# A corrected table of transfer and copy durations in the planner that interleaves a hybrid decoder step's streams

## The chip, the cores and the metric

The kernel runs on one core of a Trainium2 chip. The metric is the device time of one execution in microseconds (us), given as the median of three runs. A separate profiled execution supplies the trace. Engines are named as the profile names them: PE is TensorE (PEld its weight loads), DVE is VectorE, ACT is ScalarE, POOL is GpSimd, and SP is the queue from which nearly all transfers (DMAs) are issued.

## The reference

One layer of a decoder trunk is computed for a prompt of 1024 tokens and for 8 single-token samples, all in float32, with a model width of 1024. In outline:

```python
def mixer_inputs(...):                       # one projection feeds two mixers
    h = rms_norm(x, norm_g) * (1.0 + scale) + shift          # scale, shift, gate = c @ w_ada + b_ada
    q, kv, nsa_g, z_a, u, v, z_b, g_a, g_b = jnp.split(h @ w_in, cuts, axis=-1)
    ...
def nsa_core(...):                           # mixer A: three attention branches
    p_c = softmax(q . kc) ; o_c = p_c @ vc                   # compressed blocks of 32 keys
    idx = top_k(block importance from p_c, 8) ; o_s          # 8 selected blocks of 64 keys
    o_w = softmax over the last 512 keys                     # sliding window
    ...
def spatial_mix(vn, w_s, b_s):               # mixer B: tril(w_s) @ v_norm + b_s inside chunks of 128
    ...
def mixer_output(...):
    o_a = gw[..., 0] * o_c + gw[..., 1] * o_s + gw[..., 2] * o_w      # per head, sigmoid gates
    a = (o_a * silu(z_a)) @ w_br_a
    b = (u * s_b * silu(z_b)) @ w_br_b
    m = sigmoid(g_a) * a + sigmoid(g_b) * b
    return x + gate * (m @ w_out)
```

The samples attend to paged caches of 1024 earlier tokens; the new key and value rows are outputs as well.

## The kernel before, in words

Each float32 operand of a large product is split into a high and a low half (names ending in `h` and `l`), and a product is the three matmuls high by high, low by high, and high by low. The order of all instructions is fixed while the program is built: no scheduler reorders anything afterwards, and on each engine and each queue the instructions run in the order in which they were written.

That order is set by a planner in the source, the class `Plan`. The kernel is written as about a dozen Python generators ("streams"), each of which emits some instructions and then yields, with the tile or the condition on which its next step depends. `Plan` keeps a modelled clock for each engine. `Plan.op` is called for every instruction. It takes the start as the engine's free time or the modelled end of the operands, whichever is later, adds a duration from the table in `Plan.cost`, and notes the end. For a transfer it moves a modelled bus forward by bytes over a rate and adds a latency. `Plan.go` repeatedly picks the stream whose awaited operand is ready earliest by these clocks, measured against PE's modelled clock, with a rank to break ties. Every instruction therefore shows one line in the profile, L231, the line in `Plan.engine` that passes a call on to the engine. Tiles are told apart by name.

The stages, in order of time:

1. Modulation and first projections (to about 250 us): weights are loaded as `graw`, split into `gh` and `gl`, and 128-token tiles `xt` are normalised, transposed through the PSUM bank `mx` and copied to `hx`.
2. The samples' attention ("decode", about 250 to 404 us): cache rows arrive in `gk`, are transposed into `mx` and copied to `kh`, `kl`.
3. The prompt's attention (about 404 to 810 us): 16 query tiles (two key groups by eight blocks of 128 queries). For each tile, a "front" transposes the split queries `s` into `mx`, copies them to `R` and `R2`, and computes score maxima: PE writes scores into `mx` (`mx<-L,R`) and DVE reduces them to `bm` and `wm`. Then come the scores (`st<-R,L`), the exponentials on ACT (`pt<-st`), their split (`p`), and the products with the values (`pv<-p,vv`), which I call P·V. A "close" ends each tile: ACT copies the softmax sum to `sr` and the output to `u`; a transfer spreads the sum into `s` (`s<-sr`); DVE takes its reciprocal; a transfer writes it out (`w_d<-s`), two read it back over the partitions (`f<-w_d`); POOL multiplies `u` by `f`; PE adds the compressed branch (`mx<-pgT,vc`); DVE sums (`u<-mx,u`), and two transfers store the result (`o_d<-u`). The runs of `sr`, `s` and `f` in these transfers are 32 or 512 bytes long.
4. The merge (about 810 to 965 us). Products `xh`, `xl` are made from the stored mixer rows, loaded as `zt`; they are the right-hand sides of the merge matmuls (`<-xh,c0h` and the like). The first merge group reads ten of the twelve products of branch b. The loading of `zt` begins once the last tile has been closed.
5. The output projection and the stores (to the end).

Alongside stages 2, 3 and the start of 4 runs a filler stream, `stream(jobs)`, of rank 9: 28 jobs of projections (gates, `z`, `u`) of three pieces each. A piece is 24 matmuls of 128x344 (`mm<-hh,c0h`, `mm<-hh,c0l`, `mm<-hl,c0h` and the same with `c1`), 84 pieces or 2016 matmuls in all; its result leaves by ACT (`th`) and a transfer (`t_da<-th`, `t_db<-th`). In stage 3 a pacing rule (`paced`) also limits how many pieces may have started for the share of the tiles that is done. What is left of the filler when the last tile closes runs ahead of the merge.

PSUM has two banks of each of the four tags `mm`, `st`, `pv`, `mx`. Transposes, score maxima and the compressed branch all share the two `mx` banks, so the next group in `mx` needs the reader of the group before the last to be done.

Of the kernel before, what the change touches and what calls it, by code (L numbers as in the profile page):

```python
# [11 lines left out]
BF = mybir.dt.bfloat16  # L12
# [4 lines left out]
PSUM = bass.MemoryType.PSUM  # L17
# [75 lines left out]
class Plan:  # L93
# [72 lines left out]
    def cost(self, engine, name, outs, ins, size, start):  # L166
        if engine == "pe":
            n, m, dt = ins[1].free_size(), ins[0].free_size(), ins[0].dtype
            form, passes, turn = "split", 1, 0.0
            if dt == FR and name != "transpose":  # L170
                cost = max(0.4375 * n + 7, 104 * m / 128)
                turn = {"split": 0.0, "full": 85.0, "part": 190.0}[self.form]
            elif name == "transpose" or dt == BF:
                form, passes = "full", 2 if name == "transpose" else 1
                cost = max(0.4375 * n + 7, (26 if dt == BF else 104) * m / 128)
                turn = 190.0 if self.form == "part" else 0.0
            elif m <= 64 and n > 128:
                form, passes, cost = "part", 4, 0.4375 * n * 4 * m / 128 + 3
                turn = 0.0 if self.form == "part" else 140.0
            else:  # L180
                form, passes, cost = "full", 4, max(4 * (0.4375 * n + 7), 208 * m / 128)
                turn = 190.0 if self.form == "part" else 0.0
            self.form = form
            tick = int(start // self.TICK)
            self.columns[tick] = self.columns.get(tick, 0.0) + passes * n * ins[0].partition_size() / 128
            return cost * (2 if self.cold(start) else 1) + turn
        if engine == "dve":
            plain = name == "tensor_copy" and outs[0].space == ins[0].space
            if name == "reciprocal":
                return 80 + 18 * size  # L190
            return 67 + (0.52 if plain else 1.042) * size
        if engine == "act":
            moved = ins and self.box(ins[0])[1][0] != self.box(outs[0])[1][0]
            return (280 if len(ins) > 1 else 70) + 0.834 * size + (105 if moved else 0)
        if name == "affine_select":
            return 65 + 1.4 * size
        if name == "tensor_scalar":
            return max(330 + 0.83 * size, 3.61 * size - 28)
        return (300 + 165 * size if size < 16 else 70 + 2.27 * size)

    def op(self, engine, name, outs, ins):
        size = max(x.free_size() for x in outs + ins)
        start = self.free.get(engine, 0.0)
        for x in ins:
            start = max(start, self.after(x, True, engine))
        for x in outs:
            start = max(start, self.after(x, False, engine))
        for x in ins + outs:
            if x.space == PSUM:
                start = max([start] + [y[2] for y in self.seen.get(self.box(x)[0], ()) if y[3] != engine])  # L210
        if "dma" in name:
            self.free[engine] = start + (1038.0 if engine == "pool" else 450.0)
            self.bus = max(self.bus, self.free[engine]) + outs[0].free_nbytes() * outs[0].partition_size() / 359.0
            end = self.bus + 2000.0
        else:
            cost = self.cost(engine, name, outs, ins, size, start)
            self.free[engine] = start + cost
            end = start + cost + self.LATE[engine]
            self.last = max(self.last, end + 60.0)
        for x in ins:  # L220
            self.note(x, False, end, engine)
        for x in outs:
            self.note(x, True, end, engine)
# [1812 lines left out]
```

## Time and profile before

| what | value |
|---|---|
| median of 3 runs | 1073.53 us (1072.48 to 1075.21) |
| profiled execution, own time | 1068.52 us |
| its span in the trace | 1066.8 us |
| PE busy | 1017.3 us (95%) |
| PE weight loads busy | 873.6 us (82%) |
| DVE busy | 697.2 us (65%) |
| ACT busy | 469.3 us (44%) |
| POOL busy | 308.8 us (29%) |
| mean granted TensorE clock | 0.994 |
| read from and written to memory | 98.95 MB, 30.23 MB |

The profiled execution took 5.0 us less than the median of the three runs, so a sum made inside the trace has to be carried over to the median as a difference. A duration in a timeline row covers a merged run of like instructions (x4 is four of them); the number in square brackets is how long the engine had sat idle before it and what released it. Matmuls overlap, so their spacing and not their single duration says what PE spends on one.

### The profile page before, as it was taken

How to read it: one execution, taken by the hardware profiler on the slowest of the kernel's cores; microseconds unless marked ns; L12 is line 12 of the kernel's file. 1: busy time of each engine (PE TensorE's matmuls, PEld its weight loads, DVE VectorE, ACT ScalarE, POOL GpSimd, SP SyncE). 2: the span in 40 equal slices, each digit the busy share in tenths (PEclk: the TensorE clock that was granted, in tenths of full speed). 3: DMA queues.
4: the chain of work that ended last, by engine and by line, in shares of the span. 5: the costliest groups of instructions: out<-in, count | busy, mean ns of one | idle time of the engine just before them, and what ended most of it. 6: DMA issues, size and time to landing. Idle time of an engine off the chain costs nothing. (4 is left out here: it accounts for less than half of the span.)

```text
span 1066.8 us, 16303 instructions
## 1 busy us (share of the span) xinstructions
PE 1017.3 (95%) x5587; PEld 873.6 (82%) x5587; DVE 697.2 (65%) x1507; ACT 469.3 (44%) x984; POOL 308.8 (29%) x332
## 2 busy tenths in 40 slices
PE   6899999998999999998988999999999999999998
PEld 2489987878999998887776877778789999998776
DVE  4685686445679674798888878988842354564422
ACT  4674232001323454677675776567674341232000
POOL 0462575554321100033342324433342000252000
PEclk9999999999999999999999999999999999999999
DMA  8736351203858563411220121211123666553521
GB/s 305 231 124 206 103 182 41 70 21 123 287 186 272 179 199 87 130 53 44 78 67 28 44 64 34 65 49 46 33 67 105 192 218 201 165 170 102 168 86 63
DMA packets 106311, 130.32 MB, mean 122 GB/s; under 512 B 27299, under 2 KB 71525, under 8 KB 106230
## 3 DMA queue, kind: packets, MB, share of 16 engines
q1 hardware_dynamic: 101622, 112.52, 33.7%
q0 software_dynamic: 4608, 16.78, 5.0%
q8 instruction: 44, 0.72, 0.3%
q14 instruction: 37, 0.30, 0.1%
HBM read 98.95 MB, written 30.23 MB: 121 GB/s over the span
## 5 line engine op out<-in xcount | busy, mean ns | idle before, releaser
L231 PE MATMUL pv<-p,vv 128*128 128x512 f32 (+1 forms) x396 | 111.4, 397 | 0.0
L231 ACT ACTIVATE pt<-st 128x512 f32<-128x512 f32 x132 | 78.5, 595 | 47.8 <-PE st L231 41.9
L231 PE MATMUL mm<-hh,c1h 128*128 128x344 f32 x304 | 99.5, 327 | 0.0
L231 PE MATMUL mm<-hh,c1l 128*128 128x344 f32 x304 | 97.7, 321 | 0.0
L231 PE MATMUL mm<-hl,c1h 128*128 128x344 f32 x304 | 97.7, 321 | 0.0
L231 PE MATMUL mm<-hh,c0h 128*128 128x344 f32 x296 | 96.4, 326 | 0.0
L231 PE MATMUL mm<-hh,c0l 128*128 128x344 f32 x296 | 94.6, 319 | 0.6 <-DVE c0l L231 0.6
L231 PE MATMUL mm<-hl,c0h 128*128 128x344 f32 x296 | 94.5, 319 | 0.0
L231 PE MATMUL st<-R,L 128*128 128x512 f32 (+1 forms) x264 | 86.2, 408 | 0.0
L231 PEld LDWEIGHTS pv<-p,vv 128*128 128x128 f32 (+1 forms) x396 | 66.0, 171 | 21.9 <-DVE p L231 1.5
L231 DVE TENSOR_TENSOR p<-pt,p 128x512 fp32r<-128x512 f32 x88 | 73.4, 844 | 11.2 <-ACT p L231 10.9
L231 POOL TENSOR_TENSOR p<-pt,p 128x512 fp32r<-128x512 f32 x44 | 60.1, 1366 | 62.2 <-ACT p L231 58.3
L231 PE MATMUL mx<-L,R 128*128 128x512 f32 (+3 forms) x204 | 56.6, 344 | 10.4 <-DVE wm L231 4.1
L231 ACT ACTIVATE p<-pt 128x512 fp32r<-128x512 f32 x94 | 59.1, 629 | 15.9 <-POOL pt L231 12.5
L231 PEld LDWEIGHTS mm<-hh,c1h 128*128 128x128 f32 x304 | 57.7, 190 | 2.4
L231 PEld LDWEIGHTS mm<-hh,c1l 128*128 128x128 f32 x304 | 57.6, 190 | 2.3
L231 POOL TENSOR_TENSOR m<-m,th 128x344 f32<-128x344 f32 x24 | 24.8, 1053 | 119.9 <-DMA th<-t_da 96.3
L231 POOL TENSOR_SCALAR_AFFINE_SELECT pt<-pt 128x512 f32<-128x512 f32 x40 | 27.1, 678 | 108.7 <-ACT pt L231 105.7
L231 PEld LDWEIGHTS mm<-hh,c0l 128*128 128x128 f32 x296 | 55.7, 188 | 3.3 <-DVE c0l L231 0.9
L231 PEld LDWEIGHTS mm<-hh,c0h 128*128 128x128 f32 x296 | 55.7, 188 | 2.8 <-issue 0.4
L231 PEld LDWEIGHTS mm<-hl,c1h 128*128 128x128 f32 x304 | 57.6, 189 | 0.0
L231 PEld LDWEIGHTS mx<-L,R 128*128 128x128 f32 x204 | 34.4, 188 | 26.7 <-PE mx L231 5.1
(517 smaller groups left out, 2753.0 us busy)
## 6 DMA issues: line engine op xcount, KB each, us to landing
t_db<-th SPq DMA_DIRECT2D x24, 172.0 KB
t_da<-th SPq DMA_DIRECT2D x24, 172.0 KB
th<-t_db SPq DMA_DIRECT2D x24, 172.0 KB
th<-t_da SPq DMA_DIRECT2D x24, 172.0 KB
graw<-in_w_ada_dram SPq DMA_DIRECT2D x16, 256.0 KB
araw<-in_w_ada_dram SPq DMA_DIRECT2D x16, 256.0 KB
xt<-in_x_dram SPq DMA_DIRECT2D x8, 512.0 KB
eraw<-in_w_ada_dram SPq DMA_DIRECT2D x16, 256.0 KB
```

Of the source, the lines that this page charges most:

```text
L231: r = getattr(real, name)(*args, **kw)
```

## The change

Two branches of the planner's table are altered. No instruction's operands are written differently; what the table does is to move the planner's choice of the next stream.

```diff
         if engine == "act":
-            moved = ins and self.box(ins[0])[1][0] != self.box(outs[0])[1][0]
-            return (280 if len(ins) > 1 else 70) + 0.834 * size + (105 if moved else 0)
+            if len(ins) > 1:
+                return 280 + 0.834 * size
+            p, space = outs[0].partition_size(), (ins or outs)[0].space
+            return (70 if space == PSUM else 94) + 0.834 * size + (105 if p < 128 and (p != 64 or size == 256) else 0)
...
         if "dma" in name:
-            self.free[engine] = start + (1038.0 if engine == "pool" else 450.0)
-            self.bus = max(self.bus, self.free[engine]) + outs[0].free_nbytes() * outs[0].partition_size() / 359.0
-            end = self.bus + 2000.0
+            self.free[engine] = start + (1038.0 if engine == "pool" else 500.0)
+            short = min(4 * x.ap[-1][1] for x in outs + ins[:1]) < 512
+            self.bus = max(self.bus, self.free[engine]) + outs[0].free_nbytes() * outs[0].partition_size() / (179.5 if short else 359.0)
+            end = self.bus + (4200.0 if short else 2200.0)
```

(The remaining lines of the diff write `7` as `7.0` in the PE branch, which changes no value.) In the table, in ns:

- an ACT copy of one input has a base of 70 from PSUM as before, and of 94 from SBUF (70 before);
- the extra 105 goes to copies onto fewer than 128 partitions, other than 64 partitions with a size that isn't 256; before, it went to copies that start on another partition than their source;
- issuing a transfer on SP takes 500 (450 before), and the fixed latency is 2200 (2000 before);
- a transfer whose innermost run on either side is under 512 bytes moves at half the rate and has a latency of 4200.

Both programs have the same number of instructions on each engine. What the new table moves is the order, at these places among others. The line numbers differ by three because the change adds three lines.

PE, the ninth group of transposes of `s` (its trace time before is 489.05 us). Before, it follows directly on another group in `mx`:

```order
L231 MATMUL st<-R,L_4360 128x512
L231 MATMUL st<-R_4912,L_4363 128x512
L231 MATMUL mx<-L_4360,R 128x512
L231 MATMUL mx<-main,s_5279 128x128 x4
L231 MATMUL st<-R,L_4360 128x512
```

Now:

```order
L234 MATMUL pv<-p_5433,vv_4366 128x512
L234 MATMUL mm<-hh,c0h 128x344
L234 MATMUL mm<-hh,c0l 128x344
L234 MATMUL mm<-hl,c0h 128x344
L234 MATMUL mm<-hh,c0h 128x344
L234 MATMUL mm<-hh,c0l 128x344
L234 MATMUL mm<-hl,c0h 128x344
L234 MATMUL mx<-main,s_5458 128x128 x4
L234 MATMUL st<-R,L_4360 128x512
```

Six filler matmuls and P·V now stand between the group in `mx` that came before and the transposes.

SP, the end of the attention: the read-back of the last tile's factor (`f<-w_d_4389`), the last store (`o_d<-u`), and the loads of the merge (`zt`). Before:

```order
L231 DMA o_d_94<-u 128x128
L231 DMA f<-w_d_4389 64x4x128 x2
L231 DMA t_da_137<-th 128x344 x2
L231 DMA o_d_93<-u 128x128
L231 DMA o_d_94<-u 128x128
L231 DMA zt<-z_db_130 128x344 x3
L231 DMA t_da_137<-th 128x344
L231 DMA cr<-in_w_ga_dram 128x512 x2
L231 DMA zt<-z_db_131 128x344
L231 DMA t_da_138<-th 128x344
L231 DMA zt<-z_db_131 128x344 x2
```

Now:

```order
L234 DMA o_d_94<-u 128x128
L234 DMA f<-w_d_4389 64x4x128 x2
L234 DMA t_da_139<-th 128x344
L234 DMA cr<-in_w_ga_dram 128x512 x2
L234 DMA t_da_140<-th 128x344
L234 DMA o_d_93<-u 128x128
L234 DMA o_d_94<-u 128x128
L234 DMA zt<-z_db_130 128x344 x3
L234 DMA t_da_140<-th 128x344
L234 DMA zt<-z_db_131 128x344
L234 DMA t_da_140<-th 128x344
L234 DMA cr<-in_w_br_b_dram 128x512 x2
```

`t_da` is numbered by job, so the last store now stands two to three jobs further on in the filler (among the rows of job 140 instead of job 137), and the first weights of the merge (`in_w_br_b`) follow almost at once. `f<-w_d` of the last tile stays behind the store of the tile before it.

ACT, in the first 25 us, where the split weights `gh` of the modulation and the turned tiles `hx` alternate. Before:

```order
L231 ACTIVATE hx,xss<-xt 128x1024
L231 ACTIVATE hx<-mx 128x512
L231 ACTIVATE gh<-graw 128x512 x3
L231 ACTIVATE mrow<-mm 9x512
L231 ACTIVATE hx<-mx 128x512
```

Now:

```order
L234 ACTIVATE hx,xss<-xt 128x1024
L234 ACTIVATE gh<-graw 128x512
L234 ACTIVATE hx<-mx 128x512
L234 ACTIVATE gh<-graw 128x512
L234 ACTIVATE hx<-mx 128x512
L234 ACTIVATE gh<-graw 128x512
L234 ACTIVATE mrow<-mm 9x512
```

One `gh` has moved ahead of `hx<-mx`, another in between the two, and the third behind them.

How far the filler has come at some points of the program, in matmuls of the 2016, counted in the order of PE:

| point in PE's order | before | now |
|---|---|---|
| end of the decode's values | 672 | 696 |
| first scores of the prompt | 888 | 936 |
| first scores of the last tile | 1584 | 1728 |
| last P·V | 1620 | 1764 |
| last close (`mx<-pgT,vc`) | 1710 | 1896 |
| first merge matmul | 2016 | 2016 |

Behind the last P·V stood 42 filler matmuls, the close of tile 15 of 16, 48 more, the close of the last tile, and then 306. Now there are 90, the close of tile 15, 42, the last close, and 120.

More of the change, by code (lines that the diff above doesn't have):

```diff
@@ L170, in cost @@
             if dt == FR and name != "transpose":
-                cost = max(0.4375 * n + 7, 104 * m / 128)
+                cost = max(0.4375 * n + 7.0, 104 * m / 128)
                 turn = {"split": 0.0, "full": 85.0, "part": 190.0}[self.form]
@@ L174, in cost @@
                 form, passes = "full", 2 if name == "transpose" else 1
-                cost = max(0.4375 * n + 7, (26 if dt == BF else 104) * m / 128)
+                cost = max(0.4375 * n + 7.0, (26 if dt == BF else 104) * m / 128)
                 turn = 190.0 if self.form == "part" else 0.0
@@ L180, in cost @@
             else:
-                form, passes, cost = "full", 4, max(4 * (0.4375 * n + 7), 208 * m / 128)
+                form, passes, cost = "full", 4, max(4 * (0.4375 * n + 7.0), 208 * m / 128)
                 turn = 190.0 if self.form == "part" else 0.0
```

## The prediction

> **What bounds the kernel now.** I read the page's totals first, then a table of busy time by stage, then PE's waits, and last the timeline where those waits are longest.
>
> ```profile
> span 1066.8 us, 16303 instructions
> ...
> PE 1017.3 (95%) x5587; PEld 873.6 (82%) x5587; DVE 697.2 (65%) x1507; ACT 469.3 (44%) x984; POOL 308.8 (29%) x332
> ```
>
> PE is busy for all but 49.5 us. Both programs hold the same instructions, so only that idle time can shrink or grow. The table by stage (from and to; length; busy time of PE, its weight loads, DVE, ACT, POOL; granted clock; DMA share; GB/s) tells where it lies:
>
> ```profile
> core 0: us, PE busy (x) PEld busy (x) DVE busy (x) ACT busy (x) POOL busy (x), PEclk, DMA share, GB/s
> 0.00:50.00 50.00, 38.78 (x130) 13.52 (x131) 27.81 (x59) 26.91 (x50) 12.07 (x19) 0.94 0.81 269
> 50.00:250.00 200.00, 198.41 (x1024) 169.20 (x1023) 126.07 (x298) 62.80 (x136) 104.03 (x103) 1.00 0.35 107
> 250.00:350.00 100.00, 95.43 (x615) 90.96 (x614) 71.97 (x105) 27.36 (x53) 30.41 (x30) 0.98 0.72 234
> ...
> 404.00:449.80 45.80, 42.09 (x272) 40.30 (x273) 25.43 (x67) 25.87 (x64) 1.87 (x7) 1.00 0.44 122
> 449.80:600.00 150.20, 137.66 (x734) 112.35 (x733) 132.92 (x322) 104.11 (x223) 52.16 (x60) 1.00 0.19 55
> 600.00:801.50 201.50, 192.09 (x1015) 158.81 (x1014) 161.27 (x375) 135.97 (x284) 72.74 (x78) 1.00 0.16 49
> 801.50:826.00 24.50, 24.50 (x154) 23.77 (x153) 6.44 (x11) 11.44 (x23) 6.72 (x9) 1.00 0.38 114
> 826.00:881.40 55.40, 55.40 (x354) 55.40 (x354) 23.76 (x46) 20.83 (x45) 0.18 (x1) 1.00 0.66 202
> 881.40:975.00 93.60, 92.57 (x568) 90.23 (x567) 52.57 (x95) 22.32 (x31) 24.78 (x24) 1.00 0.53 162
> ```
>
> Length less PE busy gives 11.2 us of idle time at the start, 4.6 in the decode's first part, and 3.7, 12.5 and 9.4 in the prompt's attention, together 25.6. From 801.5 to 881.4, where leftover filler runs on without a break, there is none.
>
> What ends these waits (in all, times, longest):
>
> ```profile
> PE mx L231 <- DVE bm L231: 8.7, 12, 2.3
> PE mx L231 <- DVE wm L231: 7.3, 15, 0.8
> PE mm L231 <- ACT gh L231: 7.3, 3, 5.6
> ```
>
> The attention's waits are mostly on DVE, which reduces score maxima out of one of the two `mx` banks while PE wants it for something else. Three of them on PE:
>
> ```profile
> 489.05 0.63 PE L231 MATMUL mx<-main,s 128*128 128x128 f32 x4 [0.46 <-DVE bm L231]
> ...
> 560.75 0.41 PE L231 MATMUL mx<-main,s 128*128 128x128 f32 x2 [2.30 <-DVE bm L231]
> ...
> 687.65 0.63 PE L231 MATMUL mx<-main,s 128*128 128x128 f32 x4 [0.78 <-DVE wm L231]
> ```
>
> DVE ahead of the longest:
>
> ```profile
> 557.31 2.37 DVE L231 TENSOR_TENSOR p<-pt,p 128x512 fp32r<-128x512 f32 x2
> 559.60 0.28 DVE L231 TENSOR_TENSOR mx<-mx,tri 128x128 f32<-128x128 f32 x1
> 559.92 0.69 DVE L231 TENSOR_REDUCE bm<-mx 128x8 f32<-128x512 f32 x1
> ```
>
> The maximum that PE needed stood behind two splits of `p`. PE work placed ahead of such a transpose hides the wait; where another group in `mx` comes directly before it, nothing does.
>
> **The change, as a sum.** The table's numbers only steer the order, so I cost the order. A filler matmul takes 55.40 / 354 = 0.157 us, by the row 826.00:881.40. By the list in the section on the change, 144 of them, 22.5 us, move from behind the last P·V to ahead of it. The stretch ahead grows by 22.5 us less the idle time they fill; the stretch behind shrinks by 22.5 us plus any new wait. The 22.5 cancels, so the result is minus the idle time filled, plus new waits. Four terms:
>
> *Start.* One `gh` moves ahead of `hx` on ACT:
>
> ```profile
> 20.25 0.60 ACT L231 ACTIVATE hx<-mx 128x512 f32<-128x512 f32 x1 [3.18 <-PE mx L231]
> 20.74 1.66 ACT L231 ACTIVATE gh<-graw 128x512 fp32r<-128x512 f32 x3
> ...
> 21.41 0.43 PE L231 MATMUL mm<-gh,cs 128*42 128x512 f32 x1 [0.83 <-ACT gh L231]
> ```
>
> PE's wait of 0.83 shortens by the 0.49 between the two ACT starts. The ends are -0.8 (the wait gone) and +1.7 (a later `hx` or `mrow` waiting for all three `gh`). I take -0.5: the rest of this stage's idle time waits for the first weights, which come as before.
>
> *Decode.* Its two longest waits stand before transposes of gathered rows:
>
> ```profile
> 264.92 0.63 PE L231 MATMUL mx<-main,gk 128*128 128x128 f32 x4 [2.50 <-DVE red L231]
> ...
> 281.71 0.52 PE L231 MATMUL mx<-main,gk 128*128 128x128 f32 x3 [0.93 <-DMA gk<-in_cache_k_slc_dram,idx]
> ```
>
> The new order has 42 filler matmuls where 36 stood before the first of these, 0.94 us, and 12 more before a later group. That fills 0.94 and about half of the 0.93. I take -1.5, with ends 0 and -3.4 (both waits gone).
>
> *Attention.* The filler between the first scores and the first scores of the last tile grows from 696 matmuls to 792. Does it land where PE waits? Of the 24 groups of transposes of `s`, 11 stand directly behind another group in `mx` before, and 6 now; the one at 489.05 is such a place. For each group in `mx` I also summed, from the order, the PE work since the last use of its bank. DVE needs 0.28 + 0.69 us for a mask and a reduction, plus its queue, so I call a bank covered with 1.5 to 2 us of PE work. What is missing up to 1.5 us sums to 18.3 us before and 11.6 now (37% less); up to 2 us, 46.7 and 37.6 (19.5% less). Scaling the stage's 25.6 us of idle time by these gives -9.4 and -5.0 as ends. I take -6.5, nearer the weaker one, since a wait like that at 560.75 comes from DVE's queue and moves with it.
>
> *Start of the merge.* Here cover is taken away. The chain behind the last P·V (PE, SP, DVE, SP, POOL, DVE, SP, SP, DVE, and the first merge matmul on PE):
>
> ```profile
> 809.43 0.86 PE L231 MATMUL pv<-p,vv 128*128 128x512 f32 x3
> ...
> 813.60 0.56 SPq L231 DMA_DIRECT2D s<-sr  x1
> ...
> 816.05 0.20 DVE L231 RECIPROCAL s<-s 128x8 f32<-128x8 f32 x1 [4.78 <-DMA s<-sr]
> ...
> 819.66 1.26 SPq L231 DMA_DIRECT2D f<-w_d  x2
> ...
> 823.94 1.43 POOL L231 TENSOR_TENSOR u<-u,f 128x256 f32<-128x256 f32 x2 [5.66 <-DMA f<-w_d]
> ...
> 826.21 0.42 DVE L231 TENSOR_TENSOR u<-mx,u 128x256 f32<-128x256 f32 x1 [3.04 <-POOL u L231]
> ...
> 826.66 0.80 SPq L231 DMA_DIRECT2D o_d<-u  x2
> ...
> 828.92 2.69 SPq L231 DMA_DIRECT2D zt<-z_db  x3
> ...
> 847.45 1.38 DVE L231 SCALAR_TENSOR_TENSOR xl<-zt,xh 128x344 fp32r<-128x344 f32 x3
> ...
> 873.32 0.32 PE L231 MATMUL st<-xh,c0h 128*128 128x344 f32 x1
> ```
>
> Call the end of the last P·V, 810.3, V. The close is done at 826.63, V+16.3; the first `xl` of the three from 847.45 is the tenth product, done at about 848.0, 21.3 us after the close. PE wants it at 873.3, so 25 us of slack. Now PE reaches the close of tile 15 at V+14.1 (90 x 0.157), and the last at V+20.7 (132 x 0.157). On SP the last `f` waits behind the store of tile 15, which needs that close: issued no earlier than V+16, and from there to DVE's sum it took 826.63 - 819.66 = 7.0. The last close is done at about V+23, the tenth product at V+44.5. PE has 252 filler matmuls and the two closes, and arrives at V+40.2. A new wait of about 4 us. Ends: if three products run in the 3.9 us from 828.92 to the first `xl`, nine take 12 and the tenth comes some 3 us sooner, +1.5; if a store sits 3.8 us longer behind the tanh results on SP (as PE's pieces there are 3.8 us apart), +8. I take +4.
>
> Sum: -0.5 - 1.5 - 6.5 + 4 = -4.5. The profiled execution takes 1068.52, so 1064.0 by it; the median of the runs is 5.0 higher, and the same difference gives 1069.0.
>
> The Trainium skill ("DMA: Bandwidth & Descriptors", section "Latency and other measured facts") puts a transfer's fixed cost at about 2 us whatever its size, which speaks against the new 4.2 us for short runs; the trace's `s<-sr`, 2.45 us from issue to reciprocal, agrees with the page. By it, two such hops in each close are planned some 3.5 us too late, and the sum would be about -1 instead of -4.5 if all of that came off the slack at the merge.
>
> **Rivals.**
>
> *DVE sets the attention's time; the moved filler is free.* DVE is busy 132.92 of 150.20 us and 161.27 of 201.50, more than PE's weight loads. If PE only waits there anyway, up to 15 of the 22.5 us disappear, against +4 at the merge and -1 elsewhere: -12, 1061.5. Against it: PE is itself busy for 92% and 95% of these stretches, and only part of the waits has its cover changed. Chance 0.15. The Trainium skill ("Perfetto Trace Analysis", section "Identifying the Most-Contended Engine") goes by the highest occupancy and holds matmul busy time for a poor measure of PE; by that rule DVE is the engine in those two stretches, and its time is this rival's.
>
> *A wash.* The filler lands where PE wasn't waiting, and takes the place of P·V and scores that would have come; -2 in the attention, -1 before, +4 at the merge: +1, and 1073 to 1075. For it: the reductions wait in DVE's queue behind `p`, which a later PE doesn't shorten. Chance 0.25.
>
> *Slower, by the start of the merge.* The planner believes that `s<-sr` and `f<-w_d` take 4.2 us where the trace shows 2.45 for the first, and puts the last closes later than need be. If the last sum on DVE comes at V+28 instead of V+23, the merge waits 9 to 10 us; with -3 in the attention and -1 before, +5.5: 1079. It decides from a merge wait of about 8.5 us on, with the other terms as forecast. For it: the store of tile 15 stands on SP behind `t_da<-th`, which waits for PE and ACT. Chance 0.18.
>
> **How the numbers follow.** The forecast has 0.42. About 0.3%, 3.2 us, is what a measurement of this kernel tells from no change. My -4.5 is just beyond it, so 0.04 of the forecast's chance goes to no change; of the wash, 0.21 to no change and 0.04 to slower. Faster 0.38 + 0.15 = 0.53, same 0.25, slower 0.22. The forecast's own range adds its terms' ends: -13.3 to +4.7, or 1060.2 to 1078.2. To take in most of the first and the third rival I give 1059.5 to 1079.
>
> **What would show it.** Right: PE's idle time between the first scores and the last P·V falls from about 25.6 to 19 us, with fewer waits of `mx` on `bm` and `wm`; the wait before the first `gk` transposes falls to about 1.6; and a new wait of 1.5 to 8 us stands before the first matmul with `xh`. Wrong: no wait at the merge (the tenth product is faster than I think), or an attention with as much idle time as before, or new waits at the start.

## The result, and the profile after

The changed kernel is faster: 1065.33 us (median of 7 runs) against 1070.20 for the kernel before (7 runs), a ratio of 0.9945 with a 95% interval of 0.9919 to 0.9971. A second comparison on another occasion gave 0.9957 (0.9936 to 0.9979). The forecast was -4.5 us; the medians differ by 4.9, and by 4.7 the second time. (As a time, 1069.0 us was forecast; most of the distance to 1065.33 is the kernel before itself, 1070.20 here and 1073.53 in its first three runs.) The size of the sum was right. Two of its four terms were not, and a part of the gain has no term in it, as shown below.

The same table of busy time by stage, cut at the same points of the program: the prompt's block means (`mx<-poolT,wck`), the first scores, the last P·V, the first merge matmul, the first output matmul. Before:

```profile
0.00:412.90 412.90, 394.76 (x2182) 333.74 (x2183) 268.38 (x559) 145.24 (x310) 151.42 (x160) 0.99 0.51 164
412.90:449.81 36.91, 33.35 (x218) 31.60 (x218) 21.54 (x58) 23.82 (x59) 0.81 (x2) 1.00 0.53 142
449.81:810.29 360.48, 338.53 (x1797) 279.22 (x1796) 297.19 (x700) 246.90 (x521) 127.46 (x140) 1.00 0.18 52
810.29:873.32 63.03, 63.03 (x404) 63.03 (x404) 24.27 (x48) 23.28 (x50) 4.34 (x6) 1.00 0.65 197
873.32:965.42 92.10, 91.07 (x578) 90.51 (x577) 50.06 (x90) 21.59 (x33) 22.07 (x21) 1.00 0.54 165
965.42:1066.80 101.38, 96.58 (x418) 75.55 (x416) 35.73 (x56) 8.50 (x13) 2.71 (x3) 0.99 0.33 107
```

After:

```profile
0.00:409.25 409.25, 392.75 (x2182) 334.66 (x2183) 270.75 (x559) 145.08 (x310) 148.55 (x160) 0.99 0.51 166
409.25:452.31 43.06, 41.30 (x270) 39.78 (x270) 25.75 (x71) 25.52 (x63) 0.92 (x2) 1.00 0.48 129
452.31:825.30 372.99, 353.75 (x1889) 294.90 (x1888) 292.06 (x690) 249.65 (x527) 126.73 (x140) 1.00 0.19 55
825.30:865.69 40.39, 40.39 (x261) 40.39 (x260) 9.88 (x22) 12.86 (x28) 4.33 (x6) 1.00 0.48 146
865.69:959.82 94.13, 92.16 (x578) 90.52 (x577) 61.66 (x113) 27.51 (x46) 22.59 (x21) 1.00 0.68 208
959.82:1061.20 101.38, 96.58 (x418) 75.56 (x416) 35.72 (x56) 8.60 (x13) 2.70 (x3) 1.00 0.34 108
```

Behind the last P·V, 22.64 us have gone (63.03 to 40.39), which is the 22.5 us of filler that moved. The two rows ahead of it, the attention, grew by 6.15 and 12.51, together 18.66 us, so 144 matmuls were taken in for 3.9 us less than their own time. PE's idle time in these two rows, length less busy, fell from 25.5 to 21.0 us (19 was forecast). The merge grew by 2.0. The first row shrank by 3.7, which, as the runs below show, is no more than this row moves with one order.

To compare orders with unlike amounts of filler I use one number, called *net*: the length from the block means to the last P·V, less 0.1565 us for each filler matmul in it. It is 257.5 us before and 253.6 after. Time lost to a slow clock is not taken out of it.

PE's waits after:

```profile
PE mx L234 <- DVE wm L234: 8.8, 11, 1.7
PE mm L234 <- ACT gh L234: 5.9, 2, 5.6
PE mx L234 <- DVE BT L234: 3.7, 5, 1.4
PE mx L234 <- DVE ce L234: 3.3, 3, 2.0
PE mx L234 <- DVE bm L234: 2.7, 7, 0.7
```

and three rows of those before:

```profile
PE mx L231 <- DVE u L231: 1.8, 3, 0.7
PE mx L231 <- DVE ce L231: 1.7, 2, 1.4
PE mx L231 <- DVE BT L231: 1.4, 4, 0.6
```

The waits on `bm`, 8.7 us before, fell to 2.7, and those on `u`, 1.8, have gone from the list. Much of it came back elsewhere: `wm` 7.3 to 8.8, `BT` 1.4 to 3.7, `ce` 1.7 to 3.3. (All of these lie in the attention.) The ninth group of transposes shows the first half of this, another a few microseconds later the second:

```profile
497.90 0.60 PE L234 MATMUL mx<-main,s 128*128 128x128 f32 x4
...
505.90 0.63 PE L234 MATMUL mx<-main,s 128*128 128x128 f32 x4 [2.01 <-DVE ce L234]
```

At 497.90, behind its six filler matmuls, the wait of 0.46 is gone; at 505.90, where no filler stands directly ahead, PE waits 2.01 for DVE's `ce`.

The start of the merge, on DVE, SP and PE:

```profile
848.33 0.42 DVE L234 TENSOR_TENSOR u<-mx,u 128x256 f32<-128x256 f32 x1 [7.89 <-POOL u L234]
...
868.02 0.52 DVE L234 SCALAR_TENSOR_TENSOR xl<-zt,xh 128x344 fp32r<-128x344 f32 x1 [0.68 <-ACT xh L234]
```

```profile
848.78 0.80 SPq L234 DMA_DIRECT2D o_d<-u  x2
851.01 1.27 SPq L234 DMA_DIRECT2D zt<-z_db  x3
```

```profile
865.69 0.32 PE L234 MATMUL st<-xh,c0h 128*128 128x344 f32 x1
...
866.95 0.32 PE L234 MATMUL st<-xl,c0h 128*128 128x344 f32 x1
868.04 0.42 PE L234 MATMUL st<-xh,c0h 128*128 128x344 f32 x1 [0.77 <-ACT xh L234]
```

With V = 825.3, the close is done at V+23.4, the tenth product (the `xl` at 868.02) at V+43.2, and PE arrives at V+40.4. But PE doesn't wait at once: nine matmuls of the first group read earlier products, and only the tenth at 868.04 and the two behind it need this one.

### The profile page after: what moved, and what is told of

Read it like the earlier page. It is cut to its first block, busy times and chain, and to the rows that moved or that the text cites. A ratio compares the mean times of both kernels' runs of the same rounds, so it can differ in the third digit from the quotient of the medians.

```text
span 1061.2 us, 16281 instructions
## 1 busy us (share of the span) xinstructions
PE 1016.9 (96%) x5587; PEld 875.8 (83%) x5587; DVE 695.8 (66%) x1507; ACT 469.2 (44%) x984; POOL 305.8 (29%) x332
## 4 chain that ended last, share of the span: by engine, by line
PE 69%; DVE 16%; issue 4%; ACT 4%; DMA 4%; POOL 1%; SPq 1%; DVEq 0%; POOLq 0%; ACTq 0%
PE mm L234 27%; PE pv L234 19%; PE st L234 13%; PE mx L234 10%; DVE p L234 2%; DVE wm L234 2%; DVE mx L234 2%; DVE bm L234 2%; DVE ce L234 1%; DVE red L234 1%; DVE cst L234 1%; DVE BT L234 1%; DVE s L234 1%; DVE c0l L234 1%; DMA graw<-in_w_ada_dram 1%
## 5 line engine op out<-in xcount | busy, mean ns | idle before, releaser
L234 PE MATMUL mm<-hh,c0h 128*128 128x344 f32 x328 | 108.6, 331 | 0.0
L234 PE MATMUL mm<-hh,c0l 128*128 128x344 f32 x328 | 106.1, 324 | 1.9 <-DVE c0l L234 1.9
L234 PE MATMUL mm<-hl,c0h 128*128 128x344 f32 x328 | 106.1, 324 | 0.0
L234 PE MATMUL mm<-hh,c1l 128*128 128x344 f32 x320 | 102.2, 319 | 0.0
L234 PE MATMUL mm<-hl,c1h 128*128 128x344 f32 x320 | 102.2, 319 | 0.0
L234 DVE TENSOR_TENSOR p<-pt,p 128x512 fp32r<-128x512 f32 x88 | 65.4, 751 | 11.9 <-ACT p L234 11.5
L234 PEld LDWEIGHTS mm<-hh,c0l 128*128 128x128 f32 x328 | 62.7, 191 | 4.4 <-DVE c0l L234 2.2
L234 PEld LDWEIGHTS mm<-hh,c0h 128*128 128x128 f32 x328 | 62.9, 192 | 2.6 <-issue 0.4
L234 PEld LDWEIGHTS mm<-hl,c0h 128*128 128x128 f32 x328 | 62.8, 191 | 0.0
L234 ACT ACTIVATE th<-mm 128x344 f32<-128x344 f32 x69 | 31.4, 454 | 57.5 <-PE mm L234 48.7
```

The costliest lines, as they stand in the source:

```text
L234: r = getattr(real, name)(*args, **kw)
```

## The experiments

The runs below were timed beside the kernel before. The table gives the ratio to it; then from the profiled execution the time to the block means, how much of it went to half-speed clock (the clock not granted times the length; see the last section), the net, the stretch from the last P·V to the merge less its filler ("behind"), and the merge's length; all in us.

| run | ratio (95% interval) | to block means | of it lost to clock | net | behind | merge |
|---|---|---|---|---|---|---|
| before | 1 | 412.9 | 5.1 | 257.5 | 1.1 | 92.1 |
| before again | (one run) | 413.7 | 3.4 | 256.3 | 1.1 | 91.0 |
| after | 0.9945 (0.9919 to 0.9971) | 409.2 | 3.4 | 253.6 | 0.9 | 94.1 |
| after again | 0.9957 (0.9936 to 0.9979) | 409.6 | 0 | 253.8 | 0.9 | 92.9 |
| ACT part alone | 0.9979 (0.9964 to 0.9993) | 417.4 | 8.5 | 256.4 | 1.0 | 91.1 |
| transfer part alone | 0.9962 (0.9946 to 0.9978) | 418.2 | 3.4 | 254.2 | 1.0 | 92.0 |
| earlier close | 1.0011 (0.9996 to 1.0027) | 414.8 | 5.1 | 253.2 | 7.8 | 92.6 |
| earlier close, memset on POOL | 0.9962 (0.9940 to 0.9984) | 410.3 | 0 | 253.2 | 2.5 | 94.0 |
| filler later | 1.0041 (1.0021 to 1.0061) | 414.8 | 5.1 | 260.1 | 1.0 | 91.2 |
| filler sooner, 18 held back | 1.0192 (1.0157 to 1.0227) | 417.8 | 6.8 | 274.0 | 3.2 | 91.9 |
| filler sooner, 12 held back | 0.9998 (0.9982 to 1.0015) | 417.5 | 3.4 | 256.9 | 3.0 | 92.2 |
| table nearer the trace | 0.9971 (0.9955 to 0.9987) | 413.0 | 6.8 | 254.3 | 1.0 | 94.4 |
| no extra latency for short runs | 1.0029 (1.0010 to 1.0048) | 426.3 | 8.5 | 257.6 | 0.9 | 93.4 |
| after, sooner, 12 held back | 1.0076 (1.0054 to 1.0098) | 414.4 | 5.1 | 258.4 | 6.8 | 92.6 |

(The transfer part alone has 24 filler matmuls more ahead of the block means than the kernel before, and the run without extra latency 48 more: 3.8 and 7.5 us of their times. Half-speed clock also took part of the stage of the net: 7.8 and 5.2 us in the runs with filler sooner, 3.4 with the ACT part alone, 1.4 in the last run, 1.7 in after, the transfer part alone, filler later, table nearer the trace and no extra latency, and nothing in the other five. It took 3.4 us of "behind" with the earlier close and 3.7 in the last run, and 0.7 and 1.6 with filler sooner.)

**What is steady and what isn't.** The two kernels were run again as they are.

> The changed kernel once more, on the chip of the others, as a measure of how much a trace of one kernel moves by stage from one execution to another. If the stages' shares were real: first 409 us, 43.1 from there to the first scores, 373.0 to the last P.V, 40.4 to the merge, 94.1 merge, 101.4 output, each within 1 us of the trace after. If the first stage's difference to before (3.7 us, of which only 1.6 is idle time of PE) is variation, that stage moves by 2 us or more.

> The kernel before once more, for a second trace. If the attention's stage is steady and the stages before it are not: the 397.4 us from the first matmul of the prompt's block means to the last P.V come out again within 0.5 us, and the 412.9 us ahead of them within some 3 us either way. If the attention's gain of 3.9 us is itself variation: that stage moves by 2 us or more.

The order up to the last P·V is the same in after, after again, and the two runs with an earlier close. Their net is 253.6, 253.8, 253.2 and 253.2; the two traces of before give 257.5 and 256.3, where 0.5 had been expected. So the attention's gain is real, 3.4 us between the means (256.9 and 253.5); the clock doesn't make it, since of these six only after lost any there. The merge moves by 1.1 to 1.2 us between two traces of one order (92.1 and 91.0, 94.1 and 92.9). The time to the block means is not steady: 409.2, 409.6, 414.8 and 410.3 for one order. Two of these rows, after again and the earlier close:

```profile
0.00:409.63 409.63, 392.03 (x2182) 331.86 (x2183) 271.04 (x559) 145.29 (x310) 148.63 (x160) 1.00 0.51 165
```

```profile
0.00:414.76 414.76, 395.85 (x2182) 335.68 (x2183) 270.68 (x559) 144.93 (x310) 148.91 (x160) 0.99 0.51 163
```

The same instructions took 5.1 us more, and the clock accounts for 5.1: three stretches at half speed in one, none in the other. Without what the clock took, before has 407.8 and 410.3, and the four traces of the new order 405.8, 409.6, 409.6 and 410.3. The opening shows no gain that stands out from this.

The clock is a part of the gain all the same. For every timed run the mean granted clock is on record, and length times the share not granted gives what the clock took at most: 6.9 us for the kernel before (mean of 30 runs), 4.3 and 5.2 us for the changed kernel (7 runs each; 4.7 together, with a standard error of 0.9). So up to about 2 of the 4.9 us are clock, and about 3 are not. The order decides some of this: the transfer part alone lost 3.8 us (12 runs), the last experiment below 14.9 (6 runs).

**The halves of the change.** One kernel has the new ACT lines and the old transfer lines, the other the reverse:

```diff
-            return (280 if len(ins) > 1 else 70) + 0.834 * size + (105 if moved else 0)
...
+            return (70 if space == PSUM else 94) + 0.834 * size + (105 if p < 128 and (p != 64 or size == 256) else 0)
```

> The ACT half of the change alone (transfers priced as before). In its order the filler ahead of the last P.V is 1692 matmuls (before 1620, after 1764); what is missing to 2.0 us of PE work between uses of an mx bank is 43.8 us (before 46.7, after 37.6). Theory 'cover' (the attention's gain of 3.9 us, first scores to last P.V plus the stretch ahead of them, goes by the fall of that shortfall, 9.1 us for after): -1.2 us there, some -4 in the stages before it at most, +1 or less at the merge, so 0.997 to 0.999 of before. Rival 'amount' (it goes by the filler moved ahead, 144 matmuls for after): half of 3.9, -2.0 there. Rival 'opening' (the gain is in the first 410 us, whose order this half also alters): the attention stays within 1 us of before.

```diff
-            end = self.bus + 2000.0
...
+            end = self.bus + (4200.0 if short else 2200.0)
```

> The transfer half of the change alone (ACT copies priced as before). Filler ahead of the last P.V: 1686 matmuls; shortfall to 2.0 us at the mx banks 34.6 us, less than in after (37.6). Theory 'cover': the attention gains more than in after, about -5 us, and the last close stands 204 matmuls (32 us) ahead of the merge, so that no wait is left there: 0.993 to 0.996 of before. Rival 'amount': 66 of 144 matmuls, -1.8 us in the attention, 0.996 to 0.999. Rival 'opening': nothing in the attention, and the gain only before 410 us.

Each half alone is faster than before, with net gains of 1.1 and 3.2 us against the first trace of before; the first is no more than the two traces of before differ by (1.2). "Cover" had -1.2 and -5, "amount" -2.0 and -1.8. Neither fits both, and the halves don't separate cleanly, since each gives an order of its own.

**A close that comes earlier.** Was the wait at the merge tied to the close? One number of the pacing was changed:

```diff
-    SPANS, PACE_LEAD, PACE_FRONT, PACE_REST = 132, 12, 14, 6
+    SPANS, PACE_LEAD, PACE_FRONT, PACE_REST = 132, 12, 14, 9
```

> The changed kernel with a pacing reserve of 9 pieces in place of 6. The order is the same up to the last P.V; the last two closes then stand at filler matmul 1824 in place of 1854 and 1896, with 192 matmuls (30 us) instead of 120 behind them. Theory 'the merge waits for its first products': the stretch from the first merge matmul to the first output matmul falls from 94.1 to about 92.1 us, and the span by 1 to 2 us (0.998 to 0.999 of after). Rival (the 2 us there are spread over later chunks and not tied to the close): 94 us as in after, no change.

No wait for `xh` or `xl` was left at the start of the merge, which took 92.6 us (after 94.1 and 92.9), but the kernel was as slow as before: another wait had come up, which neither theory had. PE:

```profile
852.64 0.66 PE L234 MATMUL mx<-hh,c0l 128*128 128x344 f32 x1 [4.20 <-DVE c0l L234]
```

and DVE, ahead of it:

```profile
848.92 0.42 DVE L234 TENSOR_TENSOR u<-mx,u 128x256 f32<-128x256 f32 x1 [3.75 <-POOL u L234]
851.72 0.33 DVE L234 MEMSET ms<- 128x320 f32 x1 [2.38 <-DMA o_d<-u]
851.96 1.22 DVE L234 TENSOR_TENSOR c0l<-cr,c0h 128x512 fp32r<-128x512 f32 x2
```

The filler's next weights are split on DVE (`c0l`), and in this order the split stands behind the last sum of the close and behind a memset that waits 2.4 us for the last store. PE ran dry for 4.2 us, and then ran at half speed (stage rows from 851.2 on):

```profile
851.20:858.00 6.80, 5.36 (x19) 5.36 (x20) 3.02 (x6) 1.47 (x3) 0.00 (x0) 0.50 0.78 223
858.00:864.80 6.80, 6.80 (x45) 6.80 (x45) 3.63 (x7) 4.00 (x9) 0.00 (x0) 1.00 0.56 188
```

At half speed 19 matmuls fit into the first 6.8 us, and 45 into the second. PE was busy for 5.36 of the first. The wait, 4.2 us, and half of these 5.36 together make up the 6.9 us by which "behind" exceeds that of after. To test DVE's queue as the cause, only the memset was moved to another engine:

```diff
-        dve.memset(late["ms"].bitcast(F32), 0.0)
+        pool.memset(late["ms"].bitcast(F32), 0.0)
```

> The run with the earlier close, with one more edit: the memset of ms, which there waited 2.4 us on DVE for the last store while the split of the filler's next weights (c0l) stood behind it, is issued on POOL. Theory 'DVE's queue held the weights back': PE's wait of 4.2 us behind the last P.V falls to about 1.6, and the stretch from the last P.V to the first merge matmul, less its filler, from 7.8 us to 2 to 5 (depending on whether a half-clock stretch still follows). Rival (the weights' load or ACT's half was late): 7.8 as before.

```profile
844.19 0.42 DVE L234 TENSOR_TENSOR u<-mx,u 128x256 f32<-128x256 f32 x1 [3.71 <-POOL u L234]
844.53 1.28 DVE L234 TENSOR_TENSOR c0l<-cr,c0h 128x512 fp32r<-128x512 f32 x2
```

```profile
845.26 0.43 PE L234 MATMUL mx<-hh,c0l 128*128 128x344 f32 x1 [1.30 <-DVE c0l L234]
```

The split follows the sum at once, PE waits 1.3 instead of 4.2, the clock stays up, and "behind" falls from 7.8 to 2.5 us. That the memset in DVE's queue held the weights back is shown. The length of the merge is not tied to the close alone, though: it took 94.0 us here, with no wait for `xh` or `xl` in it either, but with waits of 2.0 us for the split weights `c1h` and `c1l`. At a median of 1065.23 us this version is level with after (1065.33, 1065.67); it doesn't beat it.

**What sets the attention's gain.** Two orders from the table of before were made by one number of the planner, the margin at which filler is taken, and the pacing:

```diff
-    plan.go(until=lambda: 1 in closed)
+    plan.go(until=lambda: 1 in closed, slack=-200.0)
```

is the one with filler later; the two with filler sooner have 200.0 there, and 18 or 12 as the last number of the pacing.

> The table of before; in the attention's planning the margin by which another stream may be late before filler is taken is 200 ns instead of 100. Net time below is the stage's length less 0.1565 us for each filler matmul in it (before 257.5, after 253.6 us). Filler ahead of the last P.V: 1644 (before 1620). Groups of transposes of s directly behind another group in mx: 4 of 24 (before 11, after 6). Shortfall to 2.0 us at the mx banks: 53.2 us (before 46.7). Theory 'cover' (shortfall decides, 0.43 us for each us): net 260.3, slower by about 3 us. Rival 'places' (what counts is how many transposes stand directly behind another group): net about 252 to 254, as in after. Rival 'amount' (0.027 us for each matmul moved ahead): net 256.9.

> The table of before; filler is taken 200 ns before it would run out of other work instead of 100 ns after, and the pacing holds back 18 pieces instead of 6. Filler ahead of the last P.V: 1584, so 36 fewer than before; shortfall to 2.0 us 41.0 (before 46.7), 7 of 24 transposes directly behind another group. Theory 'cover': net 255.0 against 257.5. Rival 'amount': 258.5, no gain or a small loss. Behind the last close stand 408 matmuls (64 us), so nothing should wait at the merge; but both closes stand at the same place, as in the run with the earlier close, and DVE's split of the next filler weights may again wait behind them (4 to 7 us).

> As the last one, with 12 pieces held back. Filler ahead of the last P.V: 1728 (108 more than before), shortfall to 2.0 us 31.8, 6 of 24. Theory 'cover': net 251.1, better than after's 253.6 by 2.5 us. Rival 'amount': 254.6, worse than after. The closes stand together with 264 matmuls behind, so the same 4 to 7 us may be lost behind the last P.V.

Filler later came out as "cover" said (260.1 against 260.3, with 1.7 us of half-speed clock in it), and against "places". With 18 pieces held back "cover" is refuted: 274.0 for 255.0, and 266.2 if all of the 7.8 us of half-speed clock in that stage is left out. With 12 the run doesn't decide: 256.9 came out for 251.1, but 5.2 us of it is half-speed clock, and 251.7 would be left without. In the run with 18 pieces held back PE's idle time in the attention is 35 us against 25.5 before, and part of it is of another kind than waits at the `mx` banks: P·V (`pv`) waits for the split of `p`, 4.5 us in all there and 5.6 with 12, where the list of before has no such wait.

**Is a truer table a better one?**

```diff
-            return (70 if space == PSUM else 94) + 0.834 * size + (105 if p < 128 and (p != 64 or size == 256) else 0)
+            return (70 if space == PSUM else 94) + 0.834 * size + (105 if p in (1, 32) and size in (128, 512) and not (p == 32 and size == 512) or p == 64 and size == 256 else 0)
...
-            end = self.bus + (4200.0 if short else 2200.0)
+            end = self.bus + (2400.0 if short else 2200.0)
```

> The changed kernel with the table brought closer to the trace: the extra 105 ns for ACT copies only where the trace of before shows it (1x512, 32x128, 64x256; not 9x512, 16x128 or 32x512), and a latency of 2400 instead of 4200 for short runs (s<-sr took 2.45 us). Filler ahead of the last P.V 1698, shortfall to 2.0 us at the mx banks 45.3 (before 46.7, after 37.6), 8 of 24 transposes directly behind another group. Theory 'cover' (0.43 us of net time in the attention for each us of shortfall): net 256.9, hardly better than before, 0.998 to 1.001 of before. Rival 'truth' (a table nearer the trace gives a better order): net at or below after's 253.7, 0.995 or less of before.

```diff
-            end = self.bus + (4200.0 if short else 2200.0)
+            end = self.bus + 2200.0
```

> The changed kernel with the extra latency of short runs taken out (2200 for all); the rest of the table as in after. Filler ahead of the last P.V 1764 as in after, shortfall 39.5, 10 of 24 transposes directly behind another group; closes at 1824 and 1854, with 162 matmuls behind the last (after: 1896 and 120). Theory 'cover': net about 254.4; the rival 'places' 257. At the merge, the theory that only the last quarter of the first group waits for the tenth product gives no wait: the close stands 6.6 us earlier.

The first is faster than before but not better than after (0.9971 against 0.9945 and 0.9957, the intervals overlap); its net of 254.3 is below what "cover" gave and above what "truth" did. The second, with nothing changed from after but a price that was too high by the trace (the 2.45 us of `s<-sr`), is slower than before, though its wait at the merge is gone as expected: the net is 257.6, as in before. (The 426.3 us ahead of the block means are no sign of the order: without its 7.5 us of filler and 8.5 us of clock 410.3 are left.) A price nearer the trace made one order better than before and one worse.

**A version to beat both.** From these, an order with good cover and room behind the close:

```diff
-    SPANS, PACE_LEAD, PACE_FRONT, PACE_REST = 132, 12, 14, 6
+    SPANS, PACE_LEAD, PACE_FRONT, PACE_REST = 132, 12, 14, 12
...
-    plan.go(until=lambda: 1 in closed)
+    plan.go(until=lambda: 1 in closed, slack=100.0)
```

> The changed kernel with filler taken 100 ns ahead of need (before: 100 ns after) in the attention's planning, and 12 pieces held back instead of 6. Shortfall 35.3 (after 37.6), 2 of 24 transposes directly behind another group, 1728 filler matmuls ahead of the last P.V; 264 behind the last close, and 144 of them before the weights that DVE splits behind the close. Theory 'cover': net 252.7, 1 us better than after; no wait behind the last P.V and none at the merge, 1.3 us better: 0.997 to 0.999 of after, so 0.993 of before. Rival: the pacing that holds filler back starves PE near the end of the attention, as where 18 pieces were held back: net over 255, no better than after.

The rival's number was right: net 258.4, and 0.8% slower than before. Among PE's waits of this run are ones that the list of before doesn't have:

```profile
PE pv L234 <- ACT p L234: 4.0, 3, 2.1
PE pv L234 <- DVE p L234: 3.1, 4, 1.0
PE pv L234 <- POOL p L234: 1.5, 1, 1.5
```

P·V waits for the split of `p` itself, 8.6 us in all. That is another wait than the one that "cover" counts. That it comes where the pacing forbids filler fits the rival, but no run separates the pacing from the margin. In the timed runs the clock took 14.9 us, and 6.6 from the kernel before beside it (28 runs). The difference, 8.2 us, is as large as the 7.3 by which this version is slower.

## Why the prediction was right, and where it wasn't

*The sum's form held.* The filler that moved cancels (22.64 us behind the last P·V, where 22.5 were worked out), and what is left is idle time filled against new waits.

*Start and decode (-2.0).* The first traces give -3.7. Between the means of two and of four traces it is -2.3, and all of that goes away with the clock's share. Of the two decode waits, the one of 2.50 fell to 2.2 (1.6 was forecast) and the one of 0.93 rose to 1.4. These terms can't be called right or wrong; the step that failed is to take a stage that moves by 5 us with one order as if it stood still. The clock has no term in the sum at all, and up to about 2 us of the gain are clock.

*Attention (-6.5, at least -5.0).* Too large: 3.4 us, and idle time down to 21.0 us in after (22.9 in after again) where 19 was forecast. The step that failed is the scaling of all 25.6 us of idle time by the fall of a count from the order. The waits that the count is about, on `bm`, did fall by 6.0; but those on `wm`, `BT` and `ce` rose by 5.4; a DVE that is busy for 292.06 of 372.99 us can make PE wait at the next place. The experiments say more: as a rule for other orders the count fails. It came within 1 us in two of the eight, in two others with the clock's share taken out, and by neither reckoning in the remaining four. What sets the gain of an order in this stage stays open.

*Start of the merge (+4, +1.5 to +8).* The chain was right to 1.3 us: the close at V+23.4 (23), the tenth product at V+43.2 (44.5), PE at V+40.4 (40.2). What was mis-sized is who needs the tenth product: nine matmuls go first, 1.4 us, and the first group lost 1.3 us (3.16 us for twelve matmuls that take 1.88). The merge as a whole grew by 2.0, and between the second traces by 2.0 as well. The rest is in part the wait for the split weights `c1h` and `c1l`, which the prediction left out: 1.2 us in after and 1.0 in after again, against 0.9 and 0.2 before.

So -4.5 came out by luck: two errors of 2 to 3 us with opposite signs, and a gain of some 2 us by the clock about where -2.0 had been forecast for the start and the decode. Attention and merge together give only -1.4; what is left of the 4.9 us beside these and the clock isn't placed, and is no more than single traces differ by. Two slips of the prediction change nothing: its terms' lower ends add up to -12.1 and not -13.3 (1061.4), and in the new table `f<-w_d`, with runs of 512 bytes, is priced as a long run; the second short hop of a close is `w_d<-s`.

The rivals: DVE as the only limit of the attention would have swallowed 15 of the 22.5 us, and 3.4 were. The Trainium skill's rule of the highest occupancy ("Perfetto Trace Analysis", section "Identifying the Most-Contended Engine") doesn't decide this stage: PE's weight loads are busy for 294.90 and DVE for 292.06 of 372.99 us after, and both wait for the other. The wash forecast -2 in the attention, nearer the 3.4 than my -6.5, but with +4 at the merge; the slower case a merge wait of 9 us, and 0.8 came. But the earlier close shows that the last closes can cost more than I had allowed, not through the merge but through DVE's queue. The rule on a transfer's fixed cost (the Trainium skill, "DMA: Bandwidth & Descriptors", section "Latency and other measured facts") fits the 2.45 us of `s<-sr` in the trace. But the sum of about -1 that the prediction worked out by it didn't come, and taking the overcharge out made the kernel slower, although the last close then came 6.6 us sooner: a wrong price was not what cost time here.

## What to carry to other kernels

A cost table that steers an order is judged by the waits that the order leaves, and not by how true its entries are; small changes of it draw new orders that are some microseconds better or worse. Filler that moves from one stage to another cancels in the sum, so count only the waits that it fills and those that it uncovers, and find for each new wait which instruction of the group really needs the late operand. Before giving a microsecond to a stage, look at how far that stage moves between two traces of the same order, and how much of it the clock took: an order that leaves waits of 2 us also pays for the slow clock behind some of them.

## What the runs showed of the hardware

PE's clock drops to half for 3.41 us after a wait, and the same wait doesn't always do it. In the trace before, at the start of the decode, behind the wait of 2.50:

```profile
265.60:269.00 3.40, 3.40 (x14) 3.34 (x13) 0.69 (x1) 0.95 (x2) 0.50 (x1) 0.50 1.02 374
269.00:272.40 3.40, 3.40 (x24) 3.21 (x23) 2.31 (x2) 1.46 (x3) 0.94 (x1) 1.00 0.49 146
```

The granted clock is 0.50 and then 1.00. Each such stretch costs up to 1.7 us; the profiled executions had from none to nine of them before the output stage. From the decode on, the 3.41 us ahead of one held 1.3 to 3.1 us of PE idle time, mostly 1.7 or more, except where one slow stretch followed directly on another (0.5 to 1.4). In after, the wait of 2.01 for `ce` at 505.90 was followed by one (from 507.2 to 510.6); in after again the same wait of 2.0 wasn't. The slow stretches fit windows of fixed length that run on by themselves. But a border that cuts the wait in two doesn't explain after again: counted back in steps of 3.4133 us from the change of the clock at 1060.73, the window from 504.36 held 1.93 us of idle time there, against 2.01 in after. What decides is open. The Trainium skill describes such windows ("TensorE: Matmul & The Clock Gate", section "What's actually happening"): a free-running window of about 3.4 us, and half rate behind an idle one. The length agrees; here less than an idle window was enough.
